# Chunked recurrence: the next chunk's first product interleaved with this chunk's outputs between two column halves

## The chip, the cores and the metric

One core of a Trainium2 chip runs the whole program. The metric is device time in microseconds, the median of three runs. A profiled execution of its own gives the trace that is read here; its time stands in the table further down.

TensorE (PE in the rows) does the matrix products and the transposes, VectorE (DVE) and ScalarE (ACT) the elementwise work, GpSimd (POOL) memsets, and the queue of SyncE (SP) loads the weights. Each engine takes its instructions in a fixed order. PE writes its results to PSUM, which has eight banks.

## The reference: what is computed

The program is two transformer-like blocks on 256 tokens. The part that changes is the RWKV-7 recurrence of the second block, for 16 heads of 64:

```
S_t = S_{t-1} diag(w_t) + (S_{t-1} a_t) b_t^T + v_t k_t^T ;  y_t = S_t r_t
...
y = (y - mean) * lax.rsqrt(var + GN_EPS)          # over the 64 values of a head
y = y.reshape(bsz, seq_len, RWKV_W) * ln_x_w + ln_x_b
```

It stands beside one large matrix product, `n @ w_in`, and is followed by another, `mix @ w_out`.

## The kernel before

The large products ("gemm" below) run as matmuls of about 258 columns that read split weights `hi` and `lo` and split activations (`Xh`, `Xl`, later `M2h`, `M2l`); they accumulate in banks called `acc`. ACT makes `hi` from the raw weights (L108), DVE makes `lo` (L109).

The recurrence is cut into five chunks of time: chunk 0 has 16 steps (padded to 32), chunks 1 to 4 have 64 each. For a chunk the kernel does, in two halves g = 0 and 1 of eight heads:

- `values`: transposes V into the lower half of the tile `UV` (PE rows `m<-ident,V`);
- `products`: the matrix `RB` of the outputs (PE rows `m<-RD,bk`), masked by DVE;
- `turn_keys`: the transposed keys `BT`;
- `state_in`: R and A times the old state `SD` (PE rows `a<-SD,ar`), then A_ak V (PE rows `a<-UV,AA`), both into a bank `a`, of which rows 0 to 63 are copied to `XQ`;
- `solve`: the small triangular solve (PE rows `a<-XQ,AA`), copied into the upper half of `UV`;
- `state_out`: the new state (PE rows `m<-UV,BT`), whose two heads of a pair are written to the two halves of the partitions in turn;
- `outputs`: RB times UV (PE rows `a<-UV,RB`) into the rows 64 to 127 of the bank `a`, copied to `yc`; then the normalisation of `yc`: a reduce, a subtraction, a square on ACT, a reduce, a reciprocal root in eleven tiny DVE instructions, a multiplication (L1334 to L1342);
- `turn`: eight transposes of `yc` on PE (rows `m<-ident,yc`), then DVE adds them into the result (`KP<-m`, L1357).

A product in float32 shows as two matmul records in the trace, so a half's eight products are 16 records.

The banks are handed out by name: `a` has two buffers, `m` has two, `acc` four. `values`, `products`, `turn_keys`, `state_out` and `turn` all take theirs from the two `m` buffers, in the order of the code.

The order comes from a table (`seq`): every step has a slot, and a slot passes with each quarter of a gemm's depth and each of its two column tiles. From this code order the compiler's own scheduler then makes each engine's fixed order, so a step may stand elsewhere than its slot. When the last `turn` has been done, the memory of the recurrence is freed; the tiles `M2h` and `M2l` of the output product lie in it.

Of the kernel before, what the change touches and what calls it, by code (L numbers as in the profile page):

```python
# [17 lines left out]
P = 128  # L18
# [24 lines left out]
class Net:  # L43
# [40 lines left out]
    def at(self, slot, fn):  # L84
        i = len(self.timed)
        while i and self.timed[i - 1][0] > slot:
            i -= 1
        self.timed.insert(i, (slot, fn))
# [810 lines left out]
    def block2_mixer(self):  # L899
        nc, a = self.nc, self.a  # L900
        v = nc.vector
# [22 lines left out]
        o, n = self.voff["mu_rwkv_2:0"]  # L924
# [26 lines left out]
        o, n = self.voff["k_a_2"]  # L951
# [14 lines left out]
        flat2 = lambda ap: ap.rearrange("p b t -> p (b t)")  # L966
# [95 lines left out]
        part = lambda f, *x: lambda: f(*x)  # L1062
        self.steps = [None, part(rates, 0), part(rates, 1), [part(rates, 2), part(rates, 3)]]
        for p2 in range(4):
# [4 lines left out]
            for i in range(2):  # L1069
                j = 2 * p2 + i  # L1070
# [124 lines left out]
        st_ = {}  # L1195
        q = lambda j: slice(j * 64, j * 64 + 64)
# [5 lines left out]
        def chunk(ci):  # L1202
            k = Chunk()
            k.C = C = 32 if ci == 0 else 64
            k.n = META if ci == 0 else 64
            c = k.c = ci - 1
            if ci == 0:
                k.bk = lambda j: flat2(bkm[:, j, :, :])
                k.ar = lambda j: flat2(arm[:, j, :, :])
                k.rr = lambda h, g: arm[h, 4 * g:4 * g + 4, 1, :]  # L1210
                k.aa = lambda e, j: AAm[:, 8 * e + j, :]
                k.v = lambda j: V[:, j, 16:80]
                k.mi = mi32
            else:
                k.bk = lambda j: flat2(bk[:, j, c, :, :])
                k.ar = lambda j: flat2(ar[:, j, c, :, :])
                k.rr = lambda h, g: ar[h, 4 * g:4 * g + 4, c, 1, :]
                k.aa = lambda e, j: AA[:, c, 8 * e + j, :]
                k.v = lambda j: V[:, j, c * 64:c * 64 + 128]
                k.mi = mi64  # L1220
            return k

        ch = [chunk(ci) for ci in range(5)]

        def open_chunks():
            c2.close()
            c5.close()
            cE.close()
            st_["cp"] = self.pool("cp", bufs=1, ctx=c3)
            st_["XQ"] = self.t(st_["cp"], [P, 8, 2, 64], "XQ")  # L1230
            st_["SD"] = self.t(st_["cp"], [P, 8, 2, 64], "SD")
            st_["RD"] = self.t(st_["cp"], [P, 4, 2, 64], "RD")
            nc.gpsimd.memset(st_["SD"], 0.0)
            nc.gpsimd.memset(st_["RD"], 0.0)

        def values(ci):
# [28 lines left out]
        def turn_keys(ci):  # L1265
# [4 lines left out]
            for g in range(2):  # L1270
# [2 lines left out]
                    self.tr(ps[:2 * C, j * P:(j + 1) * P], k.bk(4 * g + j))  # L1273
                nc.scalar.copy(BT[:, 4 * g:4 * g + 4].rearrange("p j k -> p (j k)"), ps[:2 * C, :])

        def state_in(ci, g):

            k = ch[ci]
            C = k.C
            if not g:  # L1280
                k.XY = [self.ps("a") for _ in range(2)]
                k.X = st_["XQ"][:C]
            for i in range(4):
                j = 4 * g + i
                if ci > 0:
                    self.mm(k.XY[g][:2 * C, i * P:(i + 1) * P], k.ar(j), flat2(st_["SD"][:, j]), i == 0, False)
            for i in range(8):
                j, e = 4 * g + i // 2, i % 2
                self.mm(k.XY[g][:C, q(i)], k.aa(e, j), k.UV[:, j, e, :], ci == 0 and i == 0, True)
            nc.scalar.copy(k.X[:, 4 * g:4 * g + 4], k.XY[g][:C, :].rearrange("p (j e v) -> p j e v", j=4, v=64))  # L1290

        def solve(ci, g):

            k = ch[ci]
            C = k.C
            Up = k.XY[g]
            for i in range(8):
                j, e = 4 * g + i // 2, i % 2
                self.mm(Up[:C, q(i)], k.aa(e, j)[0:C, :], k.X[:, j, e, :])
            nc.scalar.copy(k.UV[0:C, 4 * g:4 * g + 4], Up[:C, :].rearrange("p (j e v) -> p j e v", j=4, v=64))  # L1300
# [21 lines left out]
        def outputs(ci):  # L1322

            k = ch[ci]
            C, n = k.C, k.n
            rs = slice(C, C + n)
            st = [self.t(st_["cp"], [P, 8, 2], f"st{i}")[rs] for i in range(4)]
            yc = k.yc = self.t(st_["cp"], [P, 8, 2, 64], "yc")[rs]
            for g in range(2):
                for i in range(8):  # L1330
                    j, e = 4 * g + i // 2, i % 2
                    self.mm(k.XY[g][C:2 * C, q(i)], k.RB[:, j, e, :], k.UV[:, j, e, :], ci == 0 and i == 0, True)
                nc.scalar.copy(yc[:, 4 * g:4 * g + 4], k.XY[g][rs, :].rearrange("p (j e v) -> p j e v", j=4, v=64))
            v.tensor_reduce(st[0], yc, axis=AX.X, op=ALU.add)  # L1334
            v.tensor_scalar(st[0], st[0], -1.0 / 64, None, op0=ALU.mult)
            v.tensor_tensor(yc, yc, bc(st[0]), op=ALU.add)
            ysq = st_["XQ"][rs]
            nc.scalar.activation(ysq, yc, AF.Square)
            v.tensor_reduce(st[1], ysq, axis=AX.X, op=ALU.add)
            v.tensor_scalar(st[1], st[1], 1.0 / 64, GN_EPS, op0=ALU.mult, op1=ALU.add)  # L1340
            self.rsqrt(st[2], st[1], st[3])
            v.tensor_tensor(yc, yc, bc(st[2]), op=ALU.mult)  # L1342
# [63 lines left out]
        at = self.at  # L1406
        at(10, part(mixing, 3))
        at(10 + 2, fetch)
        s0, ds = 14, 4
# [4 lines left out]
        m0 = s0 + int(8 * ds)  # L1414
# [5 lines left out]
        names = ORDER.split()  # L1420
        m0 = max(m0 + 6, 0, 8 * max(i + 1 for i, x in enumerate(names) if x[0] in 'vrg') + 2)
        at(m0, open_chunks)
        at(m0, part(values, 0))
        at(m0 + 1, part(products, 0, 0))
        at(m0 + 2, part(products, 0, 1))
        at(m0 + 3, part(turn_keys, 0))
        dc = 10
        seq = "i0:0 i1:0 s0:1 s1:1 v:2 t0:2 t1:2 y:4 p0:5 p1:6 k:7 r:8"
        for ci in range(5):
            o = m0 + 3 + int(ci * dc)  # L1430
            for x in seq.split():
                nm, off = x.split(':')
                f, d, last, args = dict(i=(state_in, 0, 5, 1), s=(solve, 0, 5, 1), v=(values, 1, 5, 0),
                                        t=(state_out, 0, 4, 1), y=(outputs, 0, 5, 0), p=(products, 1, 5, 1),
                                        k=(turn_keys, 1, 4, 0), r=(turn, 0, 5, 0))[nm[0]]
                if ci + d < last:
                    at(o + float(off), part(f, ci + d, *map(int, nm[1:])))
# [15 lines left out]
        with ExitStack() as c4:  # L1453
# [53 lines left out]
            y = accs[KT - 2][0]  # L1507
# [269 lines left out]
```

## Time and profile before

| what | value |
|---|---|
| median of three runs | 2442.0 us (2440.3 to 2442.25) |
| the profiled execution's own time | 2442.96 us |
| its span in the trace | 2441.2 us |
| PE busy | 2421.8 us, 99% of the span |
| PE's granted clock, mean | 0.996 of full speed |
| DVE busy | 1646.0 us, 67% |
| ACT busy | 1132.3 us, 46% |

The recurrence's five chunks lie between about 1446 us and 1570 us of the span. Busy time of PE holds overlapping matmuls and modelled ends, so what a matmul costs is read from the distance of starts, not from its own length.

### The profile page before, as it was taken

How to read it: one execution, taken by the hardware profiler on the slowest of the kernel's cores; microseconds unless marked ns; L12 is line 12 of the kernel's file. 1: busy time of each engine (PE TensorE's matmuls, PEld its weight loads, DVE VectorE, ACT ScalarE, POOL GpSimd, SP SyncE). 2: the span in 40 equal slices, each digit the busy share in tenths (PEclk: the TensorE clock that was granted, in tenths of full speed). 3: DMA queues.
4: the chain of work that ended last, by engine and by line, in shares of the span. 5: the costliest groups of instructions: out<-in, count | busy, mean ns of one | idle time of the engine just before them, and what ended most of it. 6: DMA issues, size and time to landing. Idle time of an engine off the chain costs nothing.

```text
span 2441.2 us, 46811 instructions
## 1 busy us (share of the span) xinstructions
PE 2421.8 (99%) x19656; PEld 2349.4 (96%) x19656; DVE 1646.0 (67%) x2857; ACT 1132.3 (46%) x1574; POOL 57.6 (2%) x229
## 2 busy tenths in 40 slices
PE   9999999999999999999999999999999999999998
PEld 9999999999999999999999999999998999889986
DVE  7767667775676577577678956856865566556656
ACT  5545555443444344345664444454544444434443
POOL 3000000000000000000000000000000000000000
PEclk9999999999999999999999999999999999999999
DMA  6665456555655555656446551464555555555554
GB/s 218 186 185 166 148 164 203 185 183 177 199 189 173 194 188 176 201 179 211 143 138 197 162 145 53 139 210 156 191 189 189 185 180 188 190 189 180 184 190 138
DMA packets 402132, 431.09 MB, mean 177 GB/s; under 512 B 18849, under 2 KB 375780, under 8 KB 401456
## 3 DMA queue, kind: packets, MB, share of 16 engines
q1 hardware_dynamic: 386912, 413.41, 52.0%
q10 hardware_dynamic: 13184, 12.04, 1.6%
q0 software_dynamic: 1824, 2.64, 1.0%
q8 instruction: 154, 2.52, 0.4%
q14 instruction: 58, 0.48, 0.1%
HBM read 421.83 MB, written 6.23 MB: 175 GB/s over the span
## 4 chain that ended last, share of the span: by engine, by line
PE 93%; DVE 2%; issue 1%; DMA 0%; ACTq 0%; ACT 0%; POOL 0%; DVEq 0%; POOLq 0%
PE acc L99 85%; PE a L99 4%; PE m L99 2%; DVE lo L109 1%; PE m L104 1%; DVE sub L1111 1%; PE a L104 0%; DMA BC<-rd 0%; DVE sub L1112 0%; ACTq L1127 0%; DVE F L1737 0%; ACT hi L108 0%; DVE ar L1179 0%; DVE r L887 0%; DVE r L1182 0%
## 5 line engine op out<-in xcount | busy, mean ns | idle before, releaser
L109 DVE TENSOR_TENSOR lo<-raw,hi 128x1024 fp32r<-128x1024 f32 (+1 forms) x780 | 951.0, 1220 | 628.5 <-ACT hi L108 621.4
L108 ACT CAST hi<-raw 128x1024 fp32r<-128x1024 f32 (+1 forms) x780 | 815.6, 1046 | 1131.5 <-PE acc L99 1060.5
L99 PE MATMUL acc<-Xl,hi 128*128 128x256 f32 (+3 forms) x4296 | 1217.8, 284 | 0.2 <-DVE Xl L116 0.2
L99 PE MATMUL acc<-Xh,hi 128*128 128x256 f32 (+3 forms) x4296 | 1213.8, 283 | 3.9 <-ACT hi L108 2.1
L99 PE MATMUL acc<-Xh,lo 128*128 128x256 f32 (+3 forms) x4296 | 1215.0, 283 | 2.1 <-DVE lo L109 2.0
L99 PEld LDWEIGHTS acc<-Xh,hi 128*128 128x128 f32 x4296 | 811.0, 189 | 6.5 <-ACT hi L108 2.3
L99 PEld LDWEIGHTS acc<-Xh,lo 128*128 128x128 f32 x4296 | 812.0, 189 | 4.9 <-DVE lo L109 3.2
L99 PEld LDWEIGHTS acc<-Xl,hi 128*128 128x128 f32 x4296 | 808.7, 188 | 2.1 <-DVE Xl L116 0.5
L99 PE MATMUL acc<-ghi,lo 128*128 128x256 f32 x704 | 196.6, 280 | 0.5 <-DVE lo L109 0.5
L99 PE MATMUL acc<-glo,hi 128*128 128x256 f32 x704 | 196.7, 280 | 0.0
L99 PE MATMUL acc<-ghi,hi 128*128 128x256 f32 x704 | 196.6, 280 | 0.0
L99 PEld LDWEIGHTS acc<-ghi,lo 128*128 128x128 f32 x704 | 132.2, 188 | 0.7 <-DVE lo L109 0.7
L99 PEld LDWEIGHTS acc<-glo,hi 128*128 128x128 f32 x704 | 132.3, 188 | 0.0
L99 PEld LDWEIGHTS acc<-ghi,hi 128*128 128x128 f32 x704 | 132.3, 188 | 0.0
L99 PE MATMUL acc<-lo,ghi 128*128 128x512 f32 (+1 forms) x326 | 128.2, 394 | 0.0
L99 PE MATMUL acc<-hi,glo 128*128 128x512 f32 (+1 forms) x326 | 128.1, 393 | 0.0
L99 PE MATMUL acc<-hi,ghi 128*128 128x512 f32 (+1 forms) x326 | 116.1, 394 | 0.0
L99 PEld LDWEIGHTS acc<-hi,glo 128*128 128x128 f32 x326 | 61.1, 187 | 15.0
L99 PEld LDWEIGHTS acc<-hi,ghi 128*128 128x128 f32 x326 | 61.2, 188 | 14.5
L99 PEld LDWEIGHTS acc<-lo,ghi 128*128 128x128 f32 x326 | 61.0, 187 | 14.6
L822 DVE SCALAR_TENSOR_TENSOR fc<-fu,vt,fc 128x256 f32<-128x256 f32 x176 | 73.5, 481 | 0.0
L99 PE MATMUL acc<-M2l,hi 128*128 128x258 f32 x256 | 72.4, 284 | 0.5 <-DVE M2l L109 0.5
(492 smaller groups left out, 2300.5 us busy)
## 6 DMA issues: line engine op xcount, KB each, us to landing
raw<-in_w_in_dram SPq DMA_DIRECT2D x90, 1024.0 KB, 5.2
raw<-in_w_up_dram SPq DMA_DIRECT2D x88, 1024.0 KB, 5.1
raw<-in_w_gate_up_dram SPq DMA_DIRECT2D x87, 1024.0 KB, 5.1
raw<-in_w_down_dram SPq DMA_DIRECT2D x76, 1024.0 KB, 5.3
raw<-in_w_out_dram SPq DMA_DIRECT2D x32, 1024.0 KB, 5.5
raw<-in_w_down_dram SPq DMA_DIRECT2D x24, 512.0 KB, 3.3
Hd<-H ACTq DMA_DIRECT2D x1, 2176.0 KB, 9.6
H<-Hd ACTq DMA_DIRECT2D x1, 2176.0 KB, 9.6
```

The lines of the kernel that those rows point to most:

```text
L99: self.nc.tensor.matmul(out, lhsT, rhs, start=start, stop=stop, skip_group_check=True)
L104: self.nc.tensor.transpose(out, in_, self.ident[base:base + p, base:base + p])
L108: self.nc.scalar.copy(hi, src)
L109: self.nc.vector.tensor_sub(lo, src, hi.bitcast(F32))
L822: v.scalar_tensor_tensor(c, u[:, tp:tp + SEQ], self.vec(f"ffn_conv_w:{tp}", m), c, op0=ALU.mult, op1=ALU.add)
L1111: v.tensor_tensor(pr[:, 0:t, 0:t], Z[:, 0:t, 0:t], col, op=ALU.mult)
```

## The change

A new step `ahead(ci, g)` computes two things in turns: A_ak V of chunk `ci` (into rows 0 to 63 of the bank) and the outputs of chunk `ci - 1` (into rows 64 to 127), one product of each after the other. It takes the A_ak V products out of `state_in` and the output products and copies out of `outputs`. The two banks are taken once and kept for all chunks (`XY`), so DVE clears rows 64 to 127 after they have been read (four chunks, two banks). The table places `ahead` in slot 3 of the chunk before and the rest of `outputs` in slot 5 instead of 4.

```diff
+            st_["XY"] = [self.ps("a") for _ in range(2)]
...
+        def ahead(ci, g):
+            bank = st_["XY"][g]
+            k = ch[ci] if ci < 5 else None
+            p = ch[ci - 1] if ci else None
+            for i in range(8):
+                j, e = 4 * g + i // 2, i % 2
+                if k:
+                    self.mm(bank[:k.C, q(i)], k.aa(e, j), k.UV[:, j, e, :], i == 0, True)
+                if p:
+                    self.mm(bank[64:64 + p.C, q(i)], p.RB[:, j, e, :], p.UV[:, j, e, :], ci == 1 and i == 0, True)
+            if p:
+                rs = slice(64, 64 + p.n)
+                if not g:
+                    p.yc = self.t(st_["cp"], [P, 8, 2, 64], "yc")[rs]
+                nc.scalar.copy(p.yc[:, 4 * g:4 * g + 4], bank[rs, :].rearrange("p (j e v) -> p j e v", j=4, v=64))
+                if k:
+                    v.memset(bank[64:, :], 0.0)
...
         def state_in(ci, g):
-            if not g:
-                k.XY = [self.ps("a") for _ in range(2)]
...
-                    self.mm(k.XY[g][:2 * C, i * P:(i + 1) * P], k.ar(j), flat2(st_["SD"][:, j]), i == 0, False)
-            for i in range(8):
-                j, e = 4 * g + i // 2, i % 2
-                self.mm(k.XY[g][:C, q(i)], k.aa(e, j), k.UV[:, j, e, :], ci == 0 and i == 0, True)
+                    self.mm(bank[:2 * C, i * P:(i + 1) * P], k.ar(j), flat2(st_["SD"][:, j]), False, True)
...
         def outputs(ci):
-            for g in range(2):
-                for i in range(8):
-                    j, e = 4 * g + i // 2, i % 2
-                    self.mm(k.XY[g][C:2 * C, q(i)], k.RB[:, j, e, :], k.UV[:, j, e, :], ci == 0 and i == 0, True)
-                nc.scalar.copy(yc[:, 4 * g:4 * g + 4], k.XY[g][rs, :].rearrange("p (j e v) -> p j e v", j=4, v=64))
+            yc = k.yc
...
-        seq = "i0:0 i1:0 s0:1 s1:1 v:2 t0:2 t1:2 y:4 p0:5 p1:6 k:7 r:8"
+        seq = "i0:0 i1:0 s0:1 s1:1 v:2 t0:2 t1:2 a0:3 a1:3 y:5 p0:5 p1:6 k:7 r:8"
```

Where chunk 1 follows chunk 0, PE before has A_ak V of chunk 1 (`UV,AA`) in runs, among the state products and the transposes of `bk`:

```order
L99 MATMUL m_16916<-UV_16750,BT_16827 64x64 x8
L99 MATMUL a_17146<-SD_16746,ar_13804 128x128 x4
L99 MATMUL a_17146<-UV_16902,AA_13808 64x64
L99 MATMUL m_17052<-RD_16747,bk_13805 128x128 x4
L99 MATMUL a_17146<-UV_16902,AA_13808 64x64 x7
L104 MATMUL m_17081<-ident_64,bk_13805 128x128 x4
L99 MATMUL a_17147<-SD_16746,ar_13804 128x128 x4
L99 MATMUL a_17147<-UV_16902,AA_13808 64x64 x8
```

With the change it stands at the same place in turns with the outputs of chunk 0 (`UV,RB`), which are 32 rows by 64 and read 64 partitions, while A_ak V of chunk 1 reads 128; eight such pairs for each bank:

```order
L99 MATMUL m_16916<-UV_16752,BT_16845 64x64 x8
L99 MATMUL a_16749<-UV_16902,AA_13808 64x64
L99 MATMUL a_16749<-UV_16752,RB_16778 32x64
L99 MATMUL a_16749<-UV_16902,AA_13808 64x64
L99 MATMUL a_16749<-UV_16752,RB_16778 32x64
```

So single products of the two kinds now alternate where runs of one kind stood; in the later chunks both kinds have the same shape, 64x64 out of 128 partitions.

At the end of the recurrence, PE before has the last output products (chunk 4, second bank), then 157 gemm matmuls, then the eight transposes of that chunk's `yc`, then 15 more gemm matmuls of `w_in` before the first of the output product (`M2h`):

```order
L99 MATMUL a_18136<-UV_17888,RB_18031 64x64 x8
L99 MATMUL acc_18521<-Xh_94,lo_18525 128x260
...
L99 MATMUL acc_18642<-Xh_94,lo_18709 128x260
L104 MATMUL m_18341<-ident_64,yc_18247 128x64 x8
L99 MATMUL acc_18642<-Xh_94,hi_18708 128x260
```

With the change, PE there has six gemm matmuls, the transposes of chunk 3, one gemm matmul, the transposes of chunk 4, and then the output product:

```order
L99 MATMUL a_16750<-UV_17888,RB_18049 64x64 x8
L99 MATMUL acc_18643<-Xh_94,lo_18709 128x260
...
L104 MATMUL m_18102<-ident_64,yc_17955 128x64 x8
L99 MATMUL acc_18643<-Xh_94,lo_18709 128x260
L104 MATMUL m_18341<-ident_64,yc_18239 128x64 x8
L99 MATMUL acc_18805<-M2h_18786,hi_18809 128x258
L99 MATMUL acc_18806<-M2h_18786,hi_18809 128x258
```

The 157 matmuls between the last outputs and their transposes have moved ahead of the outputs, into the earlier chunks; seven are left.

On DVE, with the change, this stands between the addition of chunk 3's turned outputs (first row) and that of chunk 4's; the reciprocal root's eleven small rows are left out:

```order
L1368 SCALAR_TENSOR_TENSOR KP_13830<-m_18102,vt_74,KP_13830 128x64 x8
L1405 TENSOR_TENSOR hx_18768<-acc_18643,row_8_96 128x260
L109 TENSOR_TENSOR lo_18894<-raw_18891,hi_18893 128x1024
L1410 SCALAR_TENSOR_TENSOR y_18763<-hx_18760,vt_74,y_18763 128x258
L1345 TENSOR_REDUCE st_2202_18274<-yc_18239 64x16
...
L1347 TENSOR_TENSOR yc_18239<-yc_18239,st_2202_18274 64x1024
...
L1350 TENSOR_REDUCE st_2203_18275<-XQ_16745 64x16
...
L1353 TENSOR_TENSOR yc_18239<-yc_18239,st_2204_18276 64x1024
L1368 SCALAR_TENSOR_TENSOR KP_13830<-m_18341,vt_74,KP_13830 128x64 x8
L109 TENSOR_TENSOR M2l_18787<-YC_15585,M2h_18786 128x258 x8
```

Before, the same steps of chunk 4 stood between those two additions, and eight `lo` splits for coming gemm matmuls among them, where now there is one.

## Rows read from the trace of the kernel before

**Rows 1.** The page, part 1: engine, busy us (share of the span), instructions.
```profile
PE 2421.8 (99%) x19656; PEld 2349.4 (96%) x19656; DVE 1646.0 (67%) x2857; ACT 1132.3 (46%) x1574; POOL 57.6 (2%) x229
```

**Rows 2.** Waits of PE, whole span: who, for whom, total us, times, longest.
```profile
PE acc L99 <- DVE lo L109: 3.4, 7, 0.8
...
PE acc L99 <- DVE M2l L109: 0.5, 1, 0.5
```

**Rows 3.** Windows: busy us (instructions) of each engine in one stretch of the recurrence.
```profile
1460.00:1480.00 20.00, 20.00 (x227) 18.40 (x228) 13.74 (x33) 10.21 (x17) 0.94 (x1) 1.00 0.12 35
```

**Rows 4.** Timeline of PE, runs of small products: start, length, operation, records.
```profile
1445.98 0.68 PE L99 MATMUL m<-RD,bkm 128*64 128x64 f32 x8
1446.59 1.97 PE L99 MATMUL a<-UV,AAm 64*32 64x64 f32 x32
1448.49 0.68 PE L99 MATMUL m<-RD,bkm 128*64 128x64 f32 x8
...
1500.79 0.69 PE L99 MATMUL m<-UV,BT 128*64 128x64 f32 x16
1501.31 1.10 PE L99 MATMUL a<-UV,RB 128*64 128x64 f32 x16
1502.34 1.16 PE L99 MATMUL m<-RD,bk 128*128 128x128 f32 x8
...
1548.05 1.15 PE L99 MATMUL a<-UV,RB 128*64 128x64 f32 x16
1549.12 0.39 PE L99 MATMUL acc<-Xh,lo 128*128 128x260 f32 x1
```

**Rows 5.** Timeline of PE where the recurrence ends.
```profile
1568.05 0.71 PE L104 MATMUL m<-ident,yc 64*128 64x64 f32 x8
1568.69 0.39 PE L99 MATMUL acc<-Xh,hi 128*128 128x260 f32 x1
...
1570.61 0.40 PE L99 MATMUL acc<-M2h,hi 128*128 128x258 f32 x2
1571.54 0.39 PE L99 MATMUL acc<-M2l,hi 128*128 128x258 f32 x1 [0.54 <-DVE M2l L109]
```

**Rows 6.** Timeline of DVE, the normalisation of chunk 4 and what follows.
```profile
1549.84 1.22 DVE L1334 TENSOR_REDUCE st<-yc 64x16 f32<-64x1024 f32 x1 [1.44 <-ACT yc L1333]
...
1561.28 0.17 DVE L124 SCALAR_TENSOR_TENSOR st<-st 64x16 f32<-64x16 f32 x1
1561.48 0.17 DVE L125 TENSOR_TENSOR st<-st,st 64x16 f32<-64x16 f32 x1
...
1564.39 1.22 DVE L1342 TENSOR_TENSOR yc<-yc,st 64x1024 f32<-64x1024 f32 x1
1565.64 1.23 DVE L109 TENSOR_TENSOR lo<-raw,hi 128x1024 fp32r<-128x1024 f32 x1
...
1569.19 1.62 DVE L1357 SCALAR_TENSOR_TENSOR KP<-m,vt,KP 128x64 f32<-128x64 f32 x8
...
1571.06 1.10 DVE L109 TENSOR_TENSOR M2l<-YC,M2h 128x258 fp32r<-128x258 f32 x3
1572.07 0.42 DVE L1394 TENSOR_TENSOR hx<-acc,row 128x260 f32<-128x260 f32 x1
...
1575.23 0.49 DVE L1399 SCALAR_TENSOR_TENSOR y<-hx,vt,y 128x258 f32<-128x258 f32 x1
```

**Rows 7.** Timeline of ACT: the square inside the normalisation.
```profile
1554.79 1.06 ACT L1338 ACTIVATE XQ<-yc 64x1024 f32<-64x1024 f32 x1 [1.04 <-DVE yc L1336]
```

**Rows 8.** Timeline of PE around a wait before the recurrence.
```profile
1415.74 0.58 PE L99 MATMUL acc<-Xh,hi 128*128 128x260 f32 x1 [2.09 <-ACT hi L108]
...
1422.51 0.28 PE L99 MATMUL acc<-Xh,hi 128*128 128x260 f32 x1
1422.63 0.29 PE L99 MATMUL acc<-Xl,hi 128*128 128x260 f32 x1
```

**Rows 9.** Windows of the same place; the column after POOL is the granted clock.
```profile
1417.00:1420.00 3.00, 3.00 (x14) 3.00 (x15) 2.65 (x3) 0.58 (x1) 0.00 (x0) 0.50 1.45 135
```

More of the change, by code (lines that the diff above doesn't have):

```diff
@@ L1279, in state_in @@
             C = k.C
-            if not g:
-                k.XY = [self.ps("a") for _ in range(2)]
-                k.X = st_["XQ"][:C]
+            bank = st_["XY"][g]
+            k.X = st_["XQ"][:C]
             for i in range(4):
@@ L1285, in state_in @@
                 if ci > 0:
-                    self.mm(k.XY[g][:2 * C, i * P:(i + 1) * P], k.ar(j), flat2(st_["SD"][:, j]), i == 0, False)
-            for i in range(8):
-                j, e = 4 * g + i // 2, i % 2
-                self.mm(k.XY[g][:C, q(i)], k.aa(e, j), k.UV[:, j, e, :], ci == 0 and i == 0, True)
-            nc.scalar.copy(k.X[:, 4 * g:4 * g + 4], k.XY[g][:C, :].rearrange("p (j e v) -> p j e v", j=4, v=64))
+                    self.mm(bank[:2 * C, i * P:(i + 1) * P], k.ar(j), flat2(st_["SD"][:, j]), False, True)
+            nc.scalar.copy(k.X[:, 4 * g:4 * g + 4], bank[:C, :].rearrange("p (j e v) -> p j e v", j=4, v=64))
         def solve(ci, g):
@@ L1295, in solve @@
             C = k.C
-            Up = k.XY[g]
+            Up = st_["XY"][g]
             for i in range(8):
@@ L1324, in outputs @@
             k = ch[ci]
-            C, n = k.C, k.n
-            rs = slice(C, C + n)
+            rs = slice(64, 64 + k.n)
             st = [self.t(st_["cp"], [P, 8, 2], f"st{i}")[rs] for i in range(4)]
-            yc = k.yc = self.t(st_["cp"], [P, 8, 2, 64], "yc")[rs]
-            for g in range(2):
-                for i in range(8):
-                    j, e = 4 * g + i // 2, i % 2
-                    self.mm(k.XY[g][C:2 * C, q(i)], k.RB[:, j, e, :], k.UV[:, j, e, :], ci == 0 and i == 0, True)
-                nc.scalar.copy(yc[:, 4 * g:4 * g + 4], k.XY[g][rs, :].rearrange("p (j e v) -> p j e v", j=4, v=64))
+            yc = k.yc
             v.tensor_reduce(st[0], yc, axis=AX.X, op=ALU.add)
@@ L1427, in block2_mixer @@
         dc = 10
-        seq = "i0:0 i1:0 s0:1 s1:1 v:2 t0:2 t1:2 y:4 p0:5 p1:6 k:7 r:8"
+        seq = "i0:0 i1:0 s0:1 s1:1 v:2 t0:2 t1:2 a0:3 a1:3 y:5 p0:5 p1:6 k:7 r:8"
+        for g in range(2):
+            at(m0 + 1, part(ahead, 0, g))
         for ci in range(5):
@@ L1433, in block2_mixer @@
                 f, d, last, args = dict(i=(state_in, 0, 5, 1), s=(solve, 0, 5, 1), v=(values, 1, 5, 0),
-                                        t=(state_out, 0, 4, 1), y=(outputs, 0, 5, 0), p=(products, 1, 5, 1),
+                                        t=(state_out, 0, 4, 1), a=(ahead, 1, 6, 1), y=(outputs, 0, 5, 0), p=(products, 1, 5, 1),
                                         k=(turn_keys, 1, 4, 0), r=(turn, 0, 5, 0))[nm[0]]
```

## The prediction, before the run

> **What bounds the kernel now.** I read the page first: PE is busy for 2421.8 of 2441.2 us [rows 1]. Then its waits over the whole span: they are short, the two kinds shown sum to 3.9 us, and only one of them, 0.5 us, lies where the recurrence ends [rows 2]. Then a window inside the recurrence: PE is busy for all of 20 us, DVE for 13.74, ACT for 10.21 [rows 3]. So in this stage no other engine is waited for; PE works through gemm matmuls and the recurrence's small products, and the gemm covers every latency of the recurrence. Two things can therefore change the time: how long PE needs for the same products, and whether a latency that is covered now comes to lie bare. Since PE's own busy time contains overlap, I price products by distance of starts in the timeline.
>
> **The change part by part: PE's work.** A run of 16 records that all go to one column half takes 1.03 us from its start to the next run's (`UV,RB`, 1501.31 to 1502.34). The 16 records just ahead of it, `UV,BT`, which go to the two halves in turns, take 0.52 us (1500.79 to 1501.31) [rows 4]. Both have the same form, 128 partitions by 64 columns. A_ak V has it too. So alternating does what the change says: it halves the cost.
>
> - Chunks 2, 3 and 4: a pairing has 32 products, 64 records, 4 x 1.03 = 4.1 us in runs and 4 x 0.52 = 2.1 us in turns. Three pairings save 6.0 us.
> - Chunk 1 with chunk 0: here the two kinds differ in form. A_ak V reads 128 partitions into 64 columns, chunk 0's outputs 64 partitions into 32 columns. The trace shows what a change of form costs: eight `RD,bkm` records (128 by 64) take 0.61 us up to the first `UV,AAm` (64 by 32), where eight at a plain pitch, 1.90 us for 32 records, take 0.48 [rows 4]: 0.13 us. Each product of the pairing then costs 0.13 + 2 x 0.06 = 0.25 us, 32 of them 8.0 us, where runs cost 4.1: 3.9 us lost. The bounds: if the two forms overlapped as `UV,BT` does, 2.0 us would be saved; I take the row of a change between these very forms.
> - Elsewhere there are fewer changes of form, since A_ak V no longer stands in pieces between other steps. Counted in the orders, from chunk 0's first products to the first product of `M2h`: 84 changes before, 83 with the change, of which 31 lie inside the first pairing; so 32 fewer. They cost between 0.07 (the run of 1.03 us, 16 x 0.06 = 0.96) and 0.13; at 0.09, 2.9 us saved.
>
> PE's work: 6.0 - 3.9 + 2.9 = 5.0 us less.
>
> **DVE and ACT.** The copies to `yc` are only moved. The eight clearings of 64 x 512 have no row of this kind; by the nearest ones, DVE's reduce (1.22 us for 1024 elements a partition) from above and `hx` (0.42 for 260) from below [rows 6], they are 0.4 to 1.2 us each, at most 9.6 us of DVE in a stage where it is idle for 6 us of each 20 [rows 3]. What hides them is that idle time and the gemm matmuls in front of the next state product; I cost them at nothing. Without that cover each would hold `state_in` by its own length. The two standing banks take nothing from others: no other step of this stage asks for an `a` bank.
>
> **The last turn.** Here a latency comes to lie bare. In the new code the outputs of chunk i come with A_ak V of chunk i+1, which needs V of that chunk; the second `m` bank of that V is the one that the turn of chunk i-1 held. So each output step now follows the turn of the chunk before it, and the chain of normalisation and turn runs once per chunk instead of beside two. The orders show the outcome: the outputs slide back along the gemm, and after the last ones only seven gemm matmuls of 0.12 us are left, where 157 stood.
>
> Before, the last output products start at 1548.05, their transposes at 1568.05; the normalisation ends on DVE at 1565.61 (1564.39 + 1.22), 2.4 us early [rows 4 to 6]. It was covered by 19 us of gemm.
>
> With the change, the transposes of chunk 4 stand on PE ahead of every product of `M2h`, and `M2h` takes over the recurrence's memory, so nothing can pass. What they wait for, from the transposes of chunk 3 on, is DVE's row of instructions between the two additions, priced from [rows 6]: addition of chunk 3, 1.62; `hx` 0.42; `lo` 1.23; `y` 0.49; reduce 1.22; `hx` 0.42; `y` 0.49; a tiny one 0.17; `YC`, priced as `hx`, 0.42; subtraction, priced as L1342, 1.22; two `y` 0.98; `YC` 0.42; reduce 1.22; eleven tiny ones at a distance of 0.20 (1561.28 to 1561.48), 2.2; multiplication 1.22. The sum is 13.7 us. ACT's square, 1.06 [rows 7], lies beside `y`, `y` and `YC`. PE has one gemm matmul in it, some 0.2 us with its entry: it waits **13.5 us**. Bounds: below, chunk 4's own steps alone, 3 x 1.22 + 1.06 + 1.22 + 2.4 = 8.3 us; above, the 15.8 us that they took before from the reduce to the end with others' work between. I keep the sum, because it is this order's.
>
> What is late next: after those transposes DVE adds chunk 4 (1.62) and makes the first `M2l` (0.4), 2.0 us, under which PE has four `M2h` products, 0.5 us: a wait of 1.5 where it was 0.54 and 15 gemm matmuls stood in between [rows 5, 6]. 1.0 us more.
>
> **The clock.** Before the recurrence, PE waited 2.09 us; from that wait on, its granted clock is 0.50 of full speed, the lower of its two levels, 1.2 GHz, with 14 matmuls in 3 us; by 1422.51 they are 0.12 us apart again [rows 8, 9]. In those 6.8 us at 0.214 instead of 0.12 us a matmul, 3.0 us were lost. A wait of 13.5 us should bring the same; part falls under the wait for `M2l`. I take 2.0 us, between 0 and 3.0.
>
> **Sum.** -5.0 + 13.5 + 1.0 + 2.0 = +11.5 us. The profiled execution took 2442.96 us, so 2454.5; the median of the runs is 1.0 below it: **2453.5 us**. Nothing behind takes it back, since PE has no long waits there that could shrink [rows 2].
>
> **The rivals.**
>
> - *The first pairing also overlaps.* Chunk 0's outputs and chunk 1's A_ak V would run at half cost in spite of their forms: 5.9 us less, 2447.6 us. For it: they go to different column halves. Against it: the `RD,bkm` and `UV,AAm` rows [rows 4].
> - The Trainium skill, "TensorEngine Tiling (Array Packing)", Theoretical Speedup and Key Properties, gives this rival its rule: operands of at most 64 in a dimension go up to twice as fast, since different tiles work in parallel. The rows of `UV,BT` agree for one form. By that rule all four pairings would gain, 2447.6 us; Key Properties also says that a change of tiling mode, not of tile, drains the engine, and by that the first pairing loses, as in my sum.
> - *Faster.* If PE never waits at the last turn, only its saving is left: 2442.0 - 5.0 = 2437 us, down to 2431 with the first pairing overlapping too. That needs 13.7 us of work between the transposes of chunk 3 and those of chunk 4; it turns at some 5 us of bare wait, where saving and wait cancel. The order shows one matmul there.
> - *No change.* The other work between the two additions gets done earlier, the wait is the 8.3 us of the lower bound, and the first pairing overlaps: 8.2 + 1.0 + 2.0 - 10.9 = +0.3, 2442 us.
> - *More waits on the way.* Each pairing of chunks 2 to 4 needs the addition of a turn (1.62 us) before V's second half; the order leaves 26 gemm matmuls, 3.1 us, for it. If DVE is late by the length of some `lo` splits and a reduce, up to 5 us, three times, +15 us: 2468 us. For it: the chain is now in the path of each chunk. Against it: DVE is idle for 6 of 20 us.
>
> **How the numbers follow.** Forecast 0.70; first pairing overlaps 0.12; more waits 0.08; no change 0.05; faster 0.05. A difference of 0.2%, 4.9 us, is about what a measurement of this kernel can tell from none: slower 0.89, within it 0.06, faster 0.05. The range: 2446, under the rival of 2447.6, with a shorter wait; up to 2461 for the upper bounds of the wait and the clock, +2.3 and +1.0, and a few short waits on the way. It leaves out the two cases below and most of the one above.
>
> **What would show it.** The profile after should have one wait of 12 to 16 us on PE, ended by DVE's multiplication of `yc`, in front of the last `m<-ident,yc`; a window of lower granted clock behind it; runs of `UV,AA` and `UV,RB` at 0.03 us a record in three pairings and at some 0.12 in the first; and PE reaching the transposes of chunk 3 near 1565, where the same products before ended at 1570. If that wait is under 8 us or the first pairing is quick, the number is wrong; if there is no such wait, the whole forecast is.

## The result, and the profile after

| | kernel before | changed kernel |
|---|---|---|
| median | 2442.1 us (2440.3 to 2442.4, 4 runs) | 2456.3 us (2454.3 to 2460.8, 4 runs) |
| ratio, 95% interval | | 1.0058 [1.0046, 1.0069] |
| span of the profiled execution | 2441.2 us | 2458.9 us |

The change costs 14.2 us; the forecast was 11.5. The profiled execution of the changed kernel is the longest of its four, and 2.2 us of its distance to the profile of before lie ahead of the recurrence (first transposes of V at 1444.29 instead of 1442.14). In the kernels below that have the same list of gemms this point moves between 1438.7 and 1444.4, so stages are compared from there on. One execution of the last kernel below (more cover, all pairings in runs) took 6292.5 us, where its other eleven took 2434.4 to 2440.5, and is left out of its median.

The page, part 1, of the changed kernel, to be read beside [rows 1]:

```profile
PE 2422.7 (99%) x19656; PEld 2349.1 (96%) x19656; DVE 1650.6 (67%) x2865; ACT 1131.2 (46%) x1574; POOL 58.9 (2%) x229
```

The instructions are the same but for eight more on DVE, the clearings. Waits of PE, whole span (who, for whom, total us, times, longest), beside [rows 2]:

```profile
PE m L104 <- DVE yc L1353: 13.7, 1, 13.7
PE acc L99 <- DVE lo L109: 3.9, 7, 0.8
...
PE acc L99 <- ACT M2h L108: 1.0, 1, 1.0
```

The first line is new, and it is nearly as long as the whole change costs. The last is new too. Those left out lie outside of the recurrence. PE's timeline at the end of the recurrence (start, us, engine, line, operation, tiles, count, idle before and its cause), beside [rows 5]:

```profile
1570.12 0.71 PE L104 MATMUL m<-ident,yc 64*128 64x64 f32 x8
1570.76 0.39 PE L99 MATMUL acc<-Xh,lo 128*128 128x260 f32 x1
1584.81 1.08 PE L104 MATMUL m<-ident,yc 64*128 64x64 f32 x8 [13.66 <-DVE yc L1353]
1586.88 1.23 PE L99 MATMUL acc<-M2h,hi 128*128 128x258 f32 x4 [0.99 <-ACT M2h L108]
```

Between the transposes of chunk 3 and those of chunk 4 stands one gemm matmul. What DVE does in the meantime, beside [rows 6]; the dots stand for DVE's other rows, the eleven small steps of the reciprocal root among them:

```profile
1570.87 1.63 DVE L1368 SCALAR_TENSOR_TENSOR KP<-m,vt,KP 128x64 f32<-128x64 f32 x8 [1.67 <-PE m L104]
...
1574.39 1.22 DVE L1345 TENSOR_REDUCE st<-yc 64x16 f32<-64x1024 f32 x1
...
1577.16 1.22 DVE L1347 TENSOR_TENSOR yc<-yc,st 64x1024 f32<-64x1024 f32 x1
...
1579.92 1.22 DVE L1350 TENSOR_REDUCE st<-XQ 64x16 f32<-64x1024 f32 x1
...
1583.44 1.22 DVE L1353 TENSOR_TENSOR yc<-yc,st 64x1024 f32<-64x1024 f32 x1
1585.93 1.63 DVE L1368 SCALAR_TENSOR_TENSOR KP<-m,vt,KP 128x64 f32<-128x64 f32 x8 [1.27 <-PE m L104]
1587.47 2.78 DVE L109 TENSOR_TENSOR M2l<-YC,M2h 128x258 fp32r<-128x258 f32 x8
```

DVE works without a wait from 1570.87 to 1584.66, 13.8 us, where the prediction had summed 13.7.

What the prediction did not have is in the first pairing, A_ak V of chunk 1 with the outputs of chunk 0. PE's timeline there, beside [rows 4]:

```profile
1460.72 0.33 PE L99 MATMUL a<-UV,AA 128*64 128x64 f32 x2
1460.98 0.30 PE L99 MATMUL a<-UV,RB 64*32 64x64 f32 x2
1461.21 0.33 PE L99 MATMUL a<-UV,AA 128*64 128x64 f32 x2
...
1463.03 0.47 PE L99 MATMUL a<-UV,AA 128*64 128x64 f32 x2
1463.43 0.42 PE L99 MATMUL a<-UV,RB 64*32 64x64 f32 x2
1463.78 0.47 PE L99 MATMUL a<-UV,AA 128*64 128x64 f32 x2
```

Up to 1461.7 a pair of products, one of each kind, takes 0.49 us, as forecast (0.50). From 1463 on the same pair takes 0.75. The windows (stretch, its length, busy time and count of PE, PEld, DVE, ACT, POOL, then PE's granted clock, DMA share, GB/s) tell why:

```profile
1456.00:1462.00 6.00, 6.00 (x63) 4.93 (x62) 0.85 (x2) 0.86 (x2) 0.00 (x0) 1.00 0.58 175
1462.00:1469.00 7.00, 7.00 (x50) 4.59 (x49) 1.33 (x3) 0.58 (x1) 0.00 (x0) 0.50 0.01 2
1469.00:1475.60 6.60, 6.60 (x33) 5.86 (x33) 3.05 (x5) 2.92 (x5) 0.94 (x1) 0.50 0.00 0
1475.70:1482.00 6.30, 6.30 (x62) 6.07 (x61) 3.47 (x4) 3.51 (x7) 0.00 (x0) 1.00 0.00 0
```

For 13.6 us the granted clock is 0.50 of full speed, 1.2 GHz, although PE is busy for all of it. In the kernel before, the clock fell behind a wait [rows 8, 9]; here there is none.

### The profile page after: what moved, and what is told of

It reads as the page before. It is cut to its first block, busy times and chain, and to the rows that moved or that the text cites. A ratio compares the mean times of both kernels' runs of the same rounds, so it can differ in the third digit from the quotient of the medians.

```text
span 2458.9 us, 46828 instructions
## 1 busy us (share of the span) xinstructions
PE 2422.7 (99%) x19656; PEld 2349.1 (96%) x19656; DVE 1650.6 (67%) x2865; ACT 1131.2 (46%) x1574; POOL 58.9 (2%) x229
## 5 line engine op out<-in xcount | busy, mean ns | idle before, releaser
L99 PE MATMUL acc<-M2h,hi 128*128 128x258 f32 x256 | 73.9, 292 | 1.0 <-ACT M2h L108 1.0
```

The costliest lines, as they stand in the source:

```text
L99: self.nc.tensor.matmul(out, lhsT, rhs, start=start, stop=stop, skip_group_check=True)
```

## The experiments

The working theory: the 14.2 us are the uncovered last turn, plus the first pairing with its two forms and the low clock that comes of them, less what turns of equal form and fewer changes of form save. The rivals: the low clock belongs to the place and not to the turns; the wait only moves when it is covered; turns bring nothing on the path. The kernel before ran beside each group, with medians of 2442.0 to 2443.8.

**The first pairing in runs.** Chunk 1's A_ak V eight products in a row, then chunk 0's outputs eight in a row; the other pairings stay in turns.

```diff
-            for i in range(8):
+            for i, w in [(i, w) for w in "kp" for i in range(8)] if ci == 1 else [(i, w) for i in range(8) for w in "kp"]:
                 j, e = 4 * g + i // 2, i % 2
-                if k:
+                if k and w == "k":
                     self.mm(bank[:k.C, q(i)], k.aa(e, j), k.UV[:, j, e, :], i == 0, True)
-                if p:
+                if p and w == "p":
```

> Only the pairing of chunk 1 with chunk 0, whose two kinds differ in form, runs in two runs of eight instead of in turns. Theory (changing forms costs about 0.13 us a change, and this mix of forms is what brought the clock down to 0.50 from 1462.01 to 1475.66): no low clock there, 32 products in 4.1 us instead of 8 or more, and 3.9 + about 6 us less than the changed kernel, some 2446 to 2448 us. Rival 1 (forms cost this, but the clock falls at this place for another reason, since small products follow one another there): the stretch of 0.50 stays, 2452. Rival 2 (changes of form cost nothing): 2456, as the changed kernel. The wait at the last turn of 13.7 us stays in all of them.

Measured 2448.7 us, 7.6 less than the changed kernel, where the theory had 9.9. The wait of 13.7 stays. The windows of the pairing and of what follows:

```profile
1457.00:1464.00 7.00, 7.00 (x105) 6.48 (x102) 3.23 (x7) 1.80 (x4) 0.94 (x1) 1.00 0.09 29
1464.00:1471.00 7.00, 7.00 (x68) 6.77 (x67) 5.58 (x7) 5.32 (x10) 0.00 (x0) 1.00 0.00 0
```

The clock stays at 1.00 with the same products in the same place, so it is the turns that bring it down, and both rivals fall. The mean granted clock of every execution fits: 0.991 or 0.992 in the four of the changed kernel, 0.993 or 0.994 in these eight.

**All pairings in runs.** The same edit with `if True` in place of `if ci == 1`.

> All pairings stand where the change puts them, but in runs of eight of one kind, none in turns. Theory (16 records in turns take 0.52 us instead of 1.03, three pairings of equal form): 6.0 us more than the kernel with only the first pairing in runs, some 2453. Rival (the turns bring nothing on the path): the same time as that kernel.

Measured 2453.3 us, 4.6 more than with only the first pairing in runs. The turns are worth something on the path, but less than 6.0. The timeline of this kernel's second pairing shows the reason, at the border of two runs:

```profile
1483.59 0.92 PE L99 MATMUL a<-UV,AA 128*64 128x64 f32 x13
1484.30 0.27 PE L99 MATMUL a<-UV,RB 128*64 128x64 f32 x1
1484.35 0.22 PE L99 MATMUL a<-UV,AA 128*64 128x64 f32 x1
1484.40 0.22 PE L99 MATMUL a<-UV,RB 128*64 128x64 f32 x1
...
1484.46 0.22 PE L99 MATMUL a<-UV,AA 128*64 128x64 f32 x1
1484.52 0.75 PE L99 MATMUL a<-UV,RB 128*64 128x64 f32 x10
```

In the code all 16 records of `UV,AA` come first. In the trace the next run's first records, for the other column half, start ahead of the last three of this one. So runs overlap at their borders by themselves: the 64 records take 3.25 us (1483.59 to 1487.35 without the 0.5 of `UV,BT` between them), not 4.1, and turns take 2.0.

**The turn later in the ring.** One number of the table.

```diff
-        seq = "... k:7 r:8"
+        seq = "... k:7 r:13"
```

> One number of the table changes: the turn of a chunk has slot 13 instead of 8, which puts it behind the next values in the ring of two m banks, so that a pairing no longer needs the turn of two chunks ago; 137 gemm matmuls, some 16 us, then stand ahead of the last transposes. All products as in the changed kernel. Theory (the wait of 13.7 us at the last turn, the 1.0 us behind it and the low clock there are the price of the missing cover): 13.7 + 1.0 + about 3 us less than the changed kernel, 2437 to 2440 us, PE's wait for the last yc under 3 us. Rival (the waits only move, into the pairings, where the transposes of yc now stand): single waits of 2 to 5 us on yc or m in each chunk, 2448 or more.

Measured 2447.3 us, 9.0 less than the changed kernel, where 16 to 19 were expected. The wait for the last `yc` is 1.4 us instead of 13.7, and there are no new waits in the pairings: the wait went as the theory said, and it did not move, as the rival had it. The theory's time was missed by 7 us. Behind the last turn there are waits of 1.35 us for `M2h` and 1.19 for `M2l`, and a new stretch of low clock, 6.8 us; the next experiment's rows show the same. Part of the rest is scatter between executions: between the two profiles, from the first transposes of V to the end, the gain is 14.1 us. The low clock in the first pairing is there too, as it should be, here for 6.8 us.

**Both edits.**

> Both edits at once: first pairing in runs, and the turn in slot 13. If the two causes are separate, their gains add up: 2438.5 - 9.5 = some 2429 us, against 2442.1 of the kernel before. Rival 1 (the low clock in the first pairing has another cause): 2434. Rival 2 (the waits move into the pairings): 2440 or more.

Measured 2438.1 us (2435.7 to 2440.9, 11 runs), against 2442.5 of before: ratio 0.9981 [0.9972, 0.9989]. The sum of the two single gains, 7.6 + 9.0, would give 2439.7, 1.6 from what was measured, so the causes are separate. It is not the 2429 expected, and the end of the recurrence in PE's timeline shows what the cover of 137 matmuls does not hide:

```profile
1557.46 0.68 PE L104 MATMUL m<-ident,yc 64*128 64x64 f32 x8 [1.43 <-DVE yc L1353]
1559.48 0.74 PE L99 MATMUL acc<-M2h,hi 128*128 128x258 f32 x4 [1.35 <-ACT M2h L108]
1561.90 0.58 PE L99 MATMUL acc<-M2l,hi 128*128 128x258 f32 x1 [1.68 <-DVE M2l L109]
```

Three waits, 4.5 us together, and from 1561.1 on 6.8 us at a clock of 0.50.

**Which difference of form counts.** From the kernel with both edits, the second pairing is made of two forms: once with half the columns of its output products (`p.RB[:, j, e, :32]`, half of chunk 1's outputs left out), once with half their rows (`p.RB[:64]` and `p.UV[:64]`, half of each sum left out).

> From the kernel with both edits (2438.1), with the second pairing's output products cut to 32 columns (half of chunk 1's outputs are left out), so that forms 128x64 and 128x32 alternate there. Theory (a change of form costs about 0.13 us whatever the form, and many such changes in a row bring the clock down): 32 products in 8 us instead of 2.1, and a stretch of granted clock 0.50 of some 7 to 14 us: 2444 to 2450. Rival 1 (the cost is that of the form's rows alone, or of chunk 0 itself): 2438, clock 1.00. Rival 2 (the changes cost, but the clock stays): 2444.

> From the kernel with both edits (2438.1), with the second pairing's output products cut to 64 of their 128 rows (half of each sum for chunk 1's outputs is left out), so that forms 128x64 and 64x64 alternate there. Theory: as with half the columns, 2444 to 2450 with a stretch of granted clock 0.50. Rival 1 (only the columns of a form count): 2438. Rival 2 (changes cost, the clock stays): 2444.

Measured 2445.4 and 2452.7 us, with the kernel before at 2443.8 beside them, 1.3 above its time in the group of both edits. Against the kernel before of their own group, these two take 6.0 and 13.3 us more than both edits alone; the second is a little more than the theory's 6 to 12. PE's timeline of the first:

```profile
1479.14 0.33 PE L99 MATMUL a<-UV,AA 128*64 128x64 f32 x2
1479.39 0.30 PE L99 MATMUL a<-UV,RB 128*32 128x64 f32 x2
1479.62 0.33 PE L99 MATMUL a<-UV,AA 128*64 128x64 f32 x2
```

and of the second:

```profile
1479.07 0.33 PE L99 MATMUL a<-UV,AA 128*64 128x64 f32 x2
1479.33 0.33 PE L99 MATMUL a<-UV,RB 64*64 64x64 f32 x2
1479.58 0.33 PE L99 MATMUL a<-UV,AA 128*64 128x64 f32 x2
```

Up to the next pair it takes 0.48 us in the first and 0.51 in the second, where equal forms in the same place take 0.11: a change of form costs about the same whether rows or columns differ. The clock tells them apart. With half the columns it stays (windows of that kernel):

```profile
1476.00:1482.00 6.00, 6.00 (x64) 4.81 (x62) 4.28 (x12) 1.63 (x2) 0.00 (x0) 1.00 0.57 175
1482.00:1489.00 7.00, 7.00 (x74) 5.48 (x73) 3.39 (x13) 1.16 (x2) 0.95 (x1) 1.00 0.01 2
```

With half the rows it falls 3.7 us into the pairing, at 1482.3, and stays low for 13.6 us:

```profile
1476.00:1482.00 6.00, 6.00 (x62) 4.99 (x61) 4.18 (x12) 1.63 (x2) 0.00 (x0) 1.00 0.55 175
1482.60:1489.00 6.40, 6.40 (x48) 5.03 (x47) 2.44 (x11) 0.58 (x1) 0.00 (x0) 0.50 0.00 0
1489.00:1496.00 7.00, 7.00 (x35) 6.33 (x34) 4.11 (x7) 1.12 (x3) 0.94 (x1) 0.50 0.01 2
1496.50:1502.00 5.50, 5.50 (x51) 5.14 (x51) 3.52 (x5) 3.73 (x6) 0.00 (x0) 1.00 0.06 7
```

So the first is rival 2, the second the theory. There is one profile of each, but the mean clocks of all executions say the same: 0.995 or 0.996 in the eleven with half the columns, 0.995 to 0.997 in the eleven of both edits, 0.992 or 0.993 in the five with half the rows.

**Turns of two.** The first pairing in runs of two products, from the kernel with both edits (`[(i + h, w) for i in range(0, 8, 2) for w in "kp" for h in range(2)]`).

> From the kernel with both edits (2438.1), with the first pairing in runs of two products instead of eight: 16 changes of form instead of 4. Theory (0.13 us a change): about 1.6 us more, 2439.7. Open is the clock: if what counts is how many changes come in a row, half as many may leave it at 1.00; if any such alternation brings it down, 2443 or more.

Measured 2442.1 us with the kernel before at 2443.8: against before, -1.8 instead of -4.4, so 2.6 more. In the trace four products take 0.71 us instead of 0.52 in runs, some 1.6 us over 32 products, and the clock stays at 1.00 in the pairing. The price of a change holds. The question of the clock is not settled: five of the eleven executions, the profiled one among them, took 2437.6 to 2440.4 us at a mean clock of 0.996 or 0.997, and the other six 2442.1 to 2444.6 at 0.995 or 0.996. Where these six lost clock, no trace shows.

**More gemm behind the recurrence.** Both edits, and b0 and b1 later in the list of gemms.

```diff
-        ORDER = "v0 v1 v2 v3 b0 b1 r0 r1 r2 r3 g c0 ..."
+        ORDER = "v0 v1 v2 v3 r0 r1 r2 r3 g b0 b1 c0 ..."
```

> The kernel with both edits (2438.1), and in the list of gemms b0 and b1 stand behind g instead of ahead of r0, so that the recurrence begins 16 slots earlier and more gemm is left behind it: 202 matmuls instead of 137 between the last two turns' transposes, and 35 instead of none between the last transposes and the first product of M2h. All products as in the changed kernel. Theory (what the kernel with both edits still loses there, waits of 1.4 + 1.3 + 1.7 us and 6.8 us at a granted clock of 0.50, is too short a cover): these waits and the low clock go, 4.4 + about 2 us, some 2432 us. Rival (b0 and b1 were the cover of the recurrence's beginning): new waits on PE before chunk 0, 2440 or more.

Measured 2434.6 us (2432.0 to 2437.0, 5 runs) against 2442.0: ratio 0.9965 [0.9952, 0.9979], the best kernel of this study. Waits of PE, whole span:

```profile
PE acc L99 <- DVE lo L109: 4.7, 11, 0.8
...
PE m L104 <- DVE yc L1353: 0.3, 1, 0.3
```

The 0.3 us for `yc` lie ahead of the transposes of chunk 1, at 1491.6. In front of those of chunk 4 there is no wait:

```profile
1559.99 0.28 PE L99 MATMUL acc<-Xh,hi 128*128 128x260 f32 x1
1560.20 0.71 PE L104 MATMUL m<-ident,yc 64*128 64x64 f32 x8
```

So none of the three waits at the end is left, and the clock no longer falls there.

**Two controls with that list.** The kernel before with the new list alone, and the kernel with more cover with all pairings in runs.

> Control: the kernel before, with only the list of gemms changed as in the last experiment (b0 and b1 behind g). Theory (the list helps the changed kernel through the cover of its tail, and the kernel before had cover enough, 157 matmuls and a wait of 0.5 us): the time of before, 2442, within 2 us. Rival (the new list saves time by itself, wherever the recurrence's products stand): 2438, as much less as the changed kernel with both edits gained from it (3.5).

> The kernel with more cover (2434.6), with the products of all pairings in runs of eight instead of in turns. Theory (turns of one form halve the products' time, and the recurrence bounds nothing else): 6.0 us more, 2440.6, or 4.6 us more, as the same edit measured without the cover, 2439.2. Rival (with the cover the turns bring nothing): 2434.6.

The first took 2446.6 us, ratio 1.0017 [1.0008, 1.0025]: the list alone costs 4 us. I had expected no change beyond 2 us. By the sums below, some 2 us of it are small products and the way into them. Its profile also has waits of PE of 1.16 us (for ACT's `hi`) and 0.76 (for DVE's `lo`) at 1307 and 1308, and a clock of 0.50 for 3.4 us behind them; the kernel before has no wait there, and the other two kernels with the new list have both. How the rest adds up stays open. So the list is no gain of its own; it helps the new code through its end. The second took 2438.9 us, 4.3 more than with turns, or 3.8 when each is held against the kernel before of its own group. The times of the two overlap (2434.4 to 2440.5 and 2432.0 to 2437.0), so the trace has to decide: 3.4 us more in small products by the sums below. The turns keep their worth with the cover, a little under the theory's 4.6.

## Why the prediction was right, and where a step of it was off

For this I summed, over the trace rows from the first transposes of V to the first product of `M2h`, the distance from each start of a small product (every matmul that is not gemm) to the next start on PE (the wait for `M2h` taken out), and beside it the whole stretch and what follows it up to the end of the span.

| kernel | first V to first `M2h` | small products in it | from `M2h` to the end |
|---|---|---|---|
| before | 128.5 | 65.8 | 870.6 |
| changed | 142.6 | 65.4 | 872.0 |
| first pairing in runs | 133.7 | 57.1 | 872.6 |
| all pairings in runs | 137.1 | 60.7 | 872.0 |
| turn later in the ring | 127.0 | 62.4 | 873.6 |
| both edits | 120.8 | 56.3 | 874.5 |
| more cover | 129.4 | 56.2 | 870.2 |
| more cover, all in runs | 132.8 | 59.6 | 869.8 |
| before, new list | 141.7 | 66.5 | 869.7 |

(The last three have 95 more gemm matmuls, some 11 us, in the first column.) In this stretch and behind it the changed kernel takes 15.5 us more than the kernel before. The prediction's terms, one by one:

- **The wait at the last turn**, 13.5 forecast: right, 13.66, ended by the instruction named, with DVE's row just as summed. That the cover decided it is shown: with 137 matmuls between the last two turns it is 1.4, with 202 there is none.
- **The later wait**, 1.0 forecast for `M2l`: it was for ACT's `M2h` instead, 0.99 where [rows 2] had 0.5 for `M2l`, so +0.5. The first products ran at half clock, and `M2l` was in time under them.
- **The clock behind the wait**, 2.0 forecast: about right. The windows of the changed kernel:

```profile
1575.00:1584.00 9.00, 0.00 (x0) 0.00 (x0) 8.33 (x22) 1.57 (x2) 0.00 (x0) 0.50 0.00 0
1584.00:1588.00 4.00, 2.21 (x13) 1.91 (x13) 2.73 (x11) 1.58 (x6) 0.00 (x0) 0.50 0.23 33
1588.00:1591.70 3.70, 3.70 (x18) 3.70 (x18) 2.25 (x7) 0.99 (x4) 0.00 (x0) 0.50 0.60 248
1591.80:1597.00 5.20, 5.20 (x37) 4.95 (x37) 2.10 (x4) 1.76 (x3) 0.00 (x0) 1.00 0.01 3
```

  From `M2h` to the end it takes 1.4 us more than before, although the wait of 0.5 has gone from there, and the last transposes took 1.08 us instead of the 0.71 of chunk 3's: 2.3 us.
- **PE's work**, -5.0 forecast: this is the step that failed. It was -0.8, for a term is missing: the low clock during the first pairing. Turned into runs, that pairing gives 8.9 us back (142.6 to 133.7), of which 3.5 are the forms (32 products at 0.245 against the 4.3 us of the runs) and so some 5.4 the clock. The three terms that the prediction had were each off by less, from the same distances of starts:
  - The three pairings of one form, -6.0 forecast: -7.4. Before, their products stand in runs apart from each other and take 13.4 us; with the change, in turns, they take 6.0. With all pairings in runs they take 9.9: of the 7.4, runs side by side, which overlap at their borders, give 3.4 and the turns 3.9.
  - Fewer changes of form elsewhere, -2.9 forecast: some -2.2, read from the kernel with the first pairing in runs. The other small products take 1.5 us less there (the last transposes at low clock taken out), and the steps from a gemm matmul to a small product 0.7 less (5.6 to 4.9 without the wait).
  - The first pairing, +3.9 forecast: +3.4 at full clock (7.8 us against the 4.4 that its products took before).

So PE's work is -7.4 - 2.2 + 3.4 + 5.4 = -0.8, and the whole -0.8 + 13.7 + 0.5 + 2.3 = 15.7, against the 15.5 of the trace and 14.2 between the medians. The forecast named the bound, the place, the instruction and the length of the wait, and the wait makes up most of the change. PE's work was 4.2 us off; that the number missed by only 2.7 is in part luck, since the profiled execution is longer than the median. The range held the result, but it had been widened for a longer wait, the clock behind it and short waits on the way, not for a low clock with PE at work. One sign failed with it: the transposes of chunk 3 were to come near 1565 and came at 1570.12, of which 2.2 us lie ahead of the recurrence. That the clearings cost nothing agrees with the rows: eight of 485 ns on DVE, and no wait of PE on them.

Of the rivals, the one in which the first pairing overlaps is refuted by the rows of 0.49 us a pair. The Trainium skill, "TensorEngine Tiling (Array Packing)", Key Properties, says that a change of tiling mode drains the engine. The traces fit this and put a price on a change of form, some 0.13 us, for rows and for columns alike. The rival with more waits on the way did not come: no pairing has a wait in the changed kernel's list. The rival that ended faster, 2437 without a wait at the last turn, did not come either. One number of the table took most of the wait away, but the time stayed at 2447.3, above the kernel before; only without the mixed forms, at 2438.1, is it near the rival.

What stays open: part of the 4 us that the list alone costs the kernel before, why alternating rows bring the clock down where alternating columns do not, and whether turns of two always leave it up.

## What to carry to other kernels

When products of one step are brought together with those of the step before, follow the ring of buffers: whatever the pair needs now has to be over for both, and the chain that used to run beside two steps runs once for each; the last link then lies bare where no work is left to cover it. Here one slot in a table decided 9 us, and the change that cost 14 us gained 4 once its turns and its cover were mended and 7 with more work left behind. Turn small products between column halves only where their forms are equal, and price a pairing from runs as they stand in the program, borders included: side by side in runs, the three pairings of one form had already won nearly half of what they won in turns.

## What the runs showed of the hardware that was not expected

- The granted clock fell to 0.50 (1.2 GHz) with PE busy throughout, when products of 128 and of 64 rows alternated one by one: in the profiles of the changed kernel (for 13.6 us), of the one with the later turn, and of the one with half the rows. It stayed at 1.00 when only the columns differed, and in the one profile with the forms alternating by two.
- In the trace the first products of a run for the other column half start before the last ones of the run that the code has ahead of it: the 64 records of four runs of equal form take 3.25 us, not four times 1.03.
- Bringing products of one form together was worth about as much as turning them between the halves: 3.4 and 3.9 us in the three pairings of one form. Of all small products, with the new list, 66.5 us fell to 59.6 by runs alone, and to 56.2 with turns.
